# Both SwiGLU openings written out as one sequence, with the norm's token factor taken from a small load, the square roots' small steps on GpSimd, and the second FFN's block factors found inside the output projection

## The chip, the cores and the metric

The kernel runs on one core of a Trainium2 chip. The metric is the device time of one execution in microseconds (us). A core has a matrix engine (PE, which reads its stationary operand through weight loads, PEld), a vector engine (DVE), an activation engine (ACT), GpSimd (POOL) and an engine whose queue issues the DMAs (SP). Every engine works its own list of instructions in order, and waits on semaphores for the others.

## The reference

One decoder layer over 1024 tokens of width 1024, in float32:

```
x = x + 0.5 * swiglu(rms_norm(x, ffn1_norm), w_gate, w_up, w_down)      # FFN 1, hidden width 2816
p = rms_norm(x, mix_norm) @ w_in                                        # latents, q, k, v, gates
x = x + (sigmoid(g_mla) * (A @ W_A) + sigmoid(g_fox) * (B @ W_B)) @ w_o # two causal attentions
x = x + 0.5 * swiglu(rms_norm(x, ffn2_norm), w_gate, w_up, w_down)      # FFN 2
rms_norm(x, g) = x * rsqrt(mean(x*x) + 1e-6) * g
swiglu(h) = (silu(h @ w_gate) * (h @ w_up)) @ w_down
```

The change concerns the start of the two FFNs and the end of `@ w_o`.

## The kernel before

Products of float32 accuracy are made of three cheaper ones. Each operand is split in a high part and the rest (low part), and `high*high + high*low + low*high` is accumulated in PSUM. In the FFNs' first product both parts are float16, so every operand is first multiplied by a power of two: one for the tokens (from the largest absolute norm weight, `gain_scale`, L449-457) and one for each block of 128 hidden columns (from the largest absolute weight, `block_scale`, L198-217, or from the largest row sum, `pair_stat`, L713-724). A largest value per partition is spread over all partitions by a tiny matmul into a PSUM tile `mx` (`spread_max`, L185-196), and five DVE steps of one column each (`pow2`, L168-181) make the factor and its inverse from it.

An FFN's opening normalizes eight tiles of 128 tokens. For each tile, `norm_parts` (L462-514) has three steps: *scale* (L484: ACT squares and sums the row; L117-L120: a square root of one column, one step on ACT and three on DVE; L486: DVE multiplies x by it and by the norm's weights into `y`), *transpose* (L491: eight PE transposes into PSUM) and *split* (L498: ACT copies the high part; for tiles 4 to 7 also a float32 copy into `raw`; L510: DVE subtracts for the low part). `start` (L312-336) writes this out for FFN 1, and `first_half` (L338-360) for tiles 4 to 7 of both FFNs, between the products of hidden block 0 (gate and up, tokens 0 to 511; `high` L362-367, `low` L369-379).

`ffn_up` (L571-645) then does block 0 for tokens 512 to 1023 (six groups of eight matmuls), block 1 for all tokens (`proj_T`: twice 48 matmuls into `psa`), and from block 2 on one block at a time by a Strassen-like scheme of seven products of 12 matmuls each (L759, `hidden_tile`; step 0 writes `pst`, step 1 a `psb` or `psg`). Its seven token operands are the first and third quarter as they are, and five sums t1 to t4 and b22 that `token_sums` (L664-706) makes on DVE (L682 to L697) and splits (L161 on ACT, L162 on DVE). Its seven weight operands (`op`) are made by `pair_sums` (L726-754): sums on GpSimd (L735-737, L748), splits on ACT (L164) and DVE (L165). The factor of block j comes from `pair_stat(j)` (L722: ACT sums absolute values over 2048 columns), an `mx` matmul in PE's list, and `pow2`.

What sets the order: inside a `with self.in_order(...)` an engine keeps the written order; elsewhere a scheduler places the instructions by its own estimates. Before, only `start` was in such a block; `first_half` for FFN 2 and all of `ffn_up` were placed by the scheduler. A pool with a fixed count of buffers per tag also orders: `stg` (loaded weights), `whi`, `wlo`, `y` and `atp` have two each. All loads are issued by SP in list order.

For block 1 everything was found late: its weights are loaded after block 0 is under way (`w1 = self.ffn_loads(name, 1)`), their largest value is taken by two DVE reductions (L205) that stand behind block 0's and the token sums' work, and only then come factor, high part (`whi`, L164) and low part (`wlo`, L165).

The output projection (`w_o`, L1704-1715) adds `mixed @ w_o` into x, 24 matmuls for each of 8 token tiles and 2 column halves, each group read out by one DVE addition (L1715). FFN 2's block 0 factor is found between its first and its second column half.

Of the kernel before, what the change touches and what calls it, by code (L numbers as in the profile page):

```python
# [64 lines left out]
class Layer:  # L65
# [46 lines left out]
    def rsqrt1(self, ss, inv_n):  # L112
# [3 lines left out]
        v = nc.vector  # L116
        v.tensor_scalar(out=a, in0=ss, scalar1=-0.5 * inv_n, scalar2=-0.5 * EPS, op0=ALU.mult, op1=ALU.add)  # L117
# [80 lines left out]
    def block_scale(self, loads, norm, engine=None):  # L198

        box = {}  # L200
        st = self.sm.tile([P, 6], F32, tag="bst", bufs=2, name="bst")

        def biggest(after=None):
            for k, w in enumerate(loads):
                self.nc.vector.tensor_reduce(  # L205
                    out=st[:, k:k + 1], in_=w.rearrange("p k n -> p (k n)"), op=ALU.max, axis=AX.X,
                    apply_absolute_value=True,
                )
                if after is not None:
                    self.follow(after)  # L210

        def spread():
            m = st[:, 5:6]
            self.spread_max(st, len(loads), m)
            box["s"], box["inv"] = self.pow2(m, 14, st[:, 2:5], norm["inv"], engine)

        return biggest, spread, box


# [10 lines left out]
    def layer(self):  # L230
# [4 lines left out]
        self.load_x(x, src, range(1))  # L235
        norm["g"] = self.gain("ffn1_norm")
# [4 lines left out]
        first = self.start(norm, loads)  # L241
# [18 lines left out]
        pending = self.ffn_up(norm, "ffn1", first, tags)  # L260
# [32 lines left out]
        self.spare = None  # L293
# [18 lines left out]
    def start(self, norm, loads):  # L312
        ET = mybir.EngineType
        nc = self.nc
        ready = lambda t: self.norm_parts(norm, t)
        with self.in_order(ET.Activation, ET.DVE, ET.PE):

            warm = self.psg("warm")
            for k in range(20):
                nc.tensor.transpose(warm[:, (k % 4) * P:(k % 4 + 1) * P], self.ident, self.ident)  # L320
            (s0, t0, c0), (s1, t1, c1), (s2, t2, c2), (s3, t3, c3) = (ready(t) for t in range(4))
            box = []
            pg, pu = self.psbg(), self.psbg()
            pair = slice(0, 256)
            a, b = (lambda o=o, k=k: self.high(o, box[k], norm["hi"][0], pair) for k, o in enumerate((pg, pu)))

            big, spread, found = self.block_scale([l[0] for l in loads], norm)
            gs = lambda: norm.update(s=self.gain_scale(norm))
            self.spare, self.turn = self.slot("wd"), 0
            w0, w1 = (  # L330
                lambda l=l, k=k: box.append(self.col_split(l, self.spare[:, k * 1024:(k + 1) * 1024], found["s"]))
                for k, l in enumerate(loads)
            )
            for f in (s0, gs, t0, s1, t1, s2, c0, big, t2, spread, s3, c1, w0, a, w1, t3, b, c2, c3):
                f()
            norm["first"] = found["inv"]
            return self.first_half(norm, box, [ready(t) for t in range(4, NT)], (pg, pu))

    def first_half(self, norm, first, parts, begun=None):


        hT = norm["hi"], norm["lo"]
        pg, pu = begun or (self.psbg(), self.psbg())
        (s4, t4, c4), (s5, t5, c5), (s6, t6, c6), (s7, t7, c7) = parts
        hi, lo = hT[0][0], hT[1][0]
        cols = slice(256 if begun else 0, HALF)
        a, b = (lambda o=o, w=w: self.high(o, w, hi, cols) for o, w in ((pg, first[0]), (pu, first[1])))
        (ca, cb), (da, db) = (self.low(o, w, hi, lo) for o, w in ((pg, first[0]), (pu, first[1])))
        norm["ops"] = sums = self.token_sums(norm)
        d = lambda: sums[3](0)  # L350
        order = (
            (s4, a, b, ca, t4, s5, s6, c4, cb, t5, s7, c5, t6, c6, da, t7, d, c7, db)
            if begun else
            (s4, a, t4, s5, s6, c4, b, t5, c5, ca, cb, t6, s7, c6, da, t7, d, c7, db)
        )
        for f in order:
            f()
        traced = self.nc.cur_bb.bb.instructions
        self.last_act = next(i.name for i in reversed(traced) if i.engine == mybir.EngineType.Activation)
        self.last_dve = next(i.name for i in reversed(traced) if i.engine == mybir.EngineType.DVE)  # L360
        return first, (pg, pu)

    def high(self, o, w, hi, cols=slice(0, HALF)):

        for k in range(KD):
            self.nc.tensor.matmul(
                o[:, cols], lhsT=w[0][:, k, :], rhs=hi.at(k, cols), start=k == 0 and cols.start == 0, stop=False
            )

    def low(self, o, w, hi, lo):  # L370
        def first():
            for k in range(KD):
                self.nc.tensor.matmul(o, lhsT=w[1][:, k, :], rhs=hi.at(k), start=False, stop=False)

        def second():
            for k in range(KD):
                self.nc.tensor.matmul(o, lhsT=w[0][:, k, :], rhs=lo.at(k), start=False, stop=k == KD - 1)

        return first, second
# [82 lines left out]
    def norm_parts(self, st, t):  # L462


# [11 lines left out]
        box = {}  # L476

        def scale():
            if st["spill"] is not None:
                nc.sync.dma_start(st["spill"][t * P:(t + 1) * P, :], xt)  # L480
            y = box["y"] = self.ring.tile([P, D], F32, tag="y", bufs=2, name="y")
            ss = self.sm.tile([P, 1], F32, tag="ss", bufs=4, name="ss")

            nc.scalar.activation(y, xt, AF.Square, accum_out=ss)  # L484
            r = self.rsqrt1(ss, 1.0 / D)
            nc.vector.scalar_tensor_tensor(out=y, in0=xt, scalar=r, in1=st["g"], op0=ALU.mult, op1=ALU.mult)  # L486
# [6 lines left out]
        def split():  # L493
            sc, ps = st["s"] if t == 0 else None, box["ps"]

            def copy(dst, src):
                if sc is None:
                    nc.scalar.copy(dst, src)  # L498
                else:
                    nc.scalar.activation(dst, src, AF.Copy, scale=sc)  # L500

            for k in (0, 4):
                copy(h.rows(k, 4, s), ps[:, k:k + 4, :])
            if t >= 4 and st["raw"] is not None:
                for k in (0, 4):
                    copy(st["raw"].rows(k, 4, s), ps[:, k:k + 4, :])
            for k in (0, 4):
                o, a, b = l.rows(k, 4, s), ps[:, k:k + 4, :], h.rows(k, 4, s)
                if sc is None:
                    nc.vector.tensor_tensor(out=o, in0=a, in1=b, op=ALU.subtract)  # L510
# [15 lines left out]
    def col_split(self, loaded, low=None, scale=None):  # L526
        st, k0 = loaded
        dt = F32R if scale is None else F16
        hi = self.ring.tile([P, 8, P], dt, tag="whi", bufs=2, name="whi")
        lo = self.ring.tile([P, 8, P], dt, tag="wlo", bufs=2, name="wlo")  # L530
        nc = self.nc
        if scale is not None and low is not None:
            scaled = low.rearrange("p (k n) -> p k n", n=P)
            nc.scalar.activation(hi, st, AF.Copy, scale=scale)
            nc.gpsimd.tensor_scalar(out=scaled, in0=st, scalar1=scale, scalar2=None, op0=ALU.mult)
            nc.gpsimd.tensor_tensor(out=lo, in0=scaled, in1=hi, op=ALU.subtract)
            return hi, lo
# [1206 lines left out]
```

## Time and profile before

| what | us |
|---|---|
| median of 3 runs (2140.96 to 2144.5) | 2143.45 |
| the profiled execution | 2142.04 |
| its span, first to last instruction | 2140.3 |
| PE busy | 2083.4 (97%) |
| DVE busy | 1340.6 (63%) |
| ACT busy | 1051.4 (49%) |
| GpSimd busy | 701.9 (33%) |

The trace is of the profiled execution, 1.74 us longer than its span. In rows of the timeline the columns are start, duration, engine, line, operation, output<-inputs, shapes and count; a bracket gives the idle time of that engine ahead of the row and what ended it. Rows of the waits give engine, tile and line that waited, the instruction waited for, and the total, the count and the longest. Rows of the windows give the stretch, its length, each engine's busy time (instructions), PE's granted clock (1.00 is full), the DMA engines' busy share and GB/s.

### The profile page before, as it was taken

Reading aid. Unit: us, or ns where it says so; the run is one execution under the profiler, and the core shown is the slowest. Engines: PE = TensorE matmul, PEld = TensorE weight load, DVE = VectorE, ACT = ScalarE, POOL = GpSimd, SP = SyncE. Lnnn points to the kernel's source line nnn. Section 1 sums busy time; section 2 is a strip of 40 time slices with the busy share of each in tenths; the row PEclk is TensorE's granted clock in tenths of the full one; section 3 lists DMA queues with packets and bytes.
Section 4 is the critical chain, followed back from the end, with each engine's and each line's share of the span. In section 5 each row is a group of like instructions: output and inputs, shape, how many; then the busy total and the mean of one; then the engine's idle time right before and its main releaser. Section 6 shows DMA issues by size and latency. Waiting matters only on the chain.

```text
span 2140.3 us, 28367 instructions
## 1 busy us (share of the span) xinstructions
PE 2083.4 (97%) x10209; PEld 1439.9 (67%) x10209; DVE 1340.6 (63%) x2337; ACT 1051.4 (49%) x1837; POOL 701.9 (33%) x723
## 2 busy tenths in 40 slices
PE   7799999999999999999999999999899999999999
PEld 4344444457888888888888888888344444448887
DVE  7654545568776787545556677853764544559765
ACT  6355555544444554356656765422455555544442
POOL 2245555474201121123333432000155555566200
PEclk8899999999999999999999999999999999999999
DMA  7133424365434377674555684641433342455432
GB/s 212 35 99 99 151 90 130 98 251 181 138 113 146 93 218 216 206 188 138 138 144 140 182 219 120 214 150 65 113 98 109 108 129 92 141 191 202 134 107 108
DMA packets 251636, 305.39 MB, mean 143 GB/s; under 512 B 17656, under 2 KB 186472, under 8 KB 251496
## 3 DMA queue, kind: packets, MB, share of 16 engines
q1 hardware_dynamic: 251496, 303.59, 46.6%
q8 instruction: 80, 1.31, 0.3%
q14 instruction: 60, 0.49, 0.1%
HBM read 205.54 MB, written 98.00 MB: 142 GB/s over the span
## 4 chain that ended last, share of the span: by engine, by line
PE 87%; DVE 5%; DMA 2%; ACT 2%; issue 1%; POOL 1%; SPq 0%; DVEq 0%; ACTq 0%; POOLq 0%
PE pst L759 19%; PE psd L906 16%; PE psb L759 11%; PE pss L1527 4%; PE psg L759 4%; PE pspt L1553 3%; PE pspv L1564 3%; PE psgate L154 3%; PE psgate L155 3%; PE psgate L156 3%; PE psb L156 2%; PE psb L154 2%; PE psb L155 2%; PE psin L154 2%; PE psin L155 2%; PE psin L156 2%
## 5 line engine op out<-in xcount | busy, mean ns | idle before, releaser
L759 PEld LDWEIGHTS <-op 128*128 128x128 f16 x3360 | 329.1, 98 | 396.3 <-ACT op L164 6.0
L906 PE MATMUL psd<-op 128*128 128x512 f32 x1680 | 383.8, 390 | 1.8 <-DVE op L162 1.8
L906 PEld LDWEIGHTS psd<-op 128*128 128x128 f32 x1680 | 315.0, 188 | 69.5 <-DVE op L162 4.0
L759 PE MATMUL pst<-s_u,op 128*128 128x512 f16 x720 | 165.4, 379 | 3.0 <-ACT op L164 2.8
L759 PE MATMUL pst<-s_v,op 128*128 128x512 f16 x720 | 165.2, 379 | 0.0
L1534 ACT ACTIVATE s_act<-pss,nm 128x128 f32<-128x128 f32 (+7 forms) x128 | 95.0, 742 | 98.3 <-DVE nm L1531 96.1
L162 DVE TENSOR_TENSOR op<-s_u,op 128x512 fp32r<-128x512 f32 x120 | 103.9, 865 | 37.8 <-ACT op L161 37.8
L161 ACT CAST op<-s_u 128x512 fp32r<-128x512 f32 x120 | 74.4, 620 | 106.3 <-PE psd L906 91.9
L165 DVE SCALAR_TENSOR_TENSOR op<-s_act,s_wd,op 128x512 f16<-128x512 f32 x100 | 83.5, 852 | 55.0 <-ACT op L164 54.9
L165 DVE SCALAR_TENSOR_TENSOR op<-s_u,s_v,op 128x512 f16<-128x512 f32 x100 | 83.4, 852 | 53.0 <-ACT op L164 52.9
L735 POOL TENSOR_TENSOR sums<-s_u 128x512 f32<-128x512 f32 x20 | 26.3, 1315 | 271.9 <-DVE bst L175 176.0
L1527 PE MATMUL pss<-s_wd 96*128 96x256 f32 (+5 forms) x480 | 113.1, 361 | 0.4 <-DMA s_wd<-mk 0.3
L161 ACT CAST op<-s_wd 128x512 fp32r<-128x512 f32 x95 | 59.0, 621 | 106.5 <-PE psd L906 97.3
L1572 DVE TENSOR_TENSOR cmb<-pspv,cmb 64x512 f32<-64x512 f32 x64 | 44.0, 688 | 104.1 <-ACT cmb L1571 103.6
L164 ACT ACTIVATE op<-s_act,s_wd 128x512 f16<-128x512 f32 x100 | 67.9, 716 | 81.5 <-DVE s_wd L178 72.8
L164 ACT ACTIVATE op<-s_u,s_v 128x512 f16<-128x512 f32 x100 | 67.8, 716 | 79.2 <-DVE s_v L178 76.4
L162 DVE TENSOR_TENSOR op<-s_wd,op 128x512 fp32r<-128x512 f32 x95 | 80.3, 845 | 36.1 <-ACT op L161 36.1
L154 PE MATMUL psgate<-s_u,whi 128*128 128x512 f32 x256 | 101.6, 397 | 0.6 <-ACT z L1376 0.6
L1557 DVE TENSOR_TENSOR s_v<-pspt,s_v 128x512 fp32r<-128x512 f32 (+1 forms) x160 | 96.4, 632 | 7.7 <-ACT s_v L1556 6.0
L155 PE MATMUL psgate<-s_u,whi 128*128 128x512 f32 x256 | 100.8, 394 | 0.0
L156 PE MATMUL psgate<-s_u,wlo 128*128 128x512 f32 x256 | 100.5, 393 | 0.0
L1531 DVE TENSOR_REDUCE nm<-pss 128x1 f32<-128x128 f32 (+7 forms) x128 | 93.6, 750 | 1.5
(521 smaller groups left out, 4664.4 us busy)
## 6 DMA issues: line engine op xcount, KB each, us to landing
sumd<-s_u SPq DMA_DIRECT2D x20, 1024.0 KB, 5.2
sumd<-s_wd SPq DMA_DIRECT2D x13, 1024.0 KB, 5.2
s_wd<-fd SPq DMA_DIRECT2D x48, 256.0 KB, 5.4
s_u<-in_ffn_w_down_dram SPq DMA_DIRECT2D x22, 512.0 KB, 5.5
s_wd<-sumd SPq DMA_DIRECT2D x14, 768.0 KB, 4.2
s_u<-sumd SPq DMA_DIRECT2D x14, 768.0 KB, 4.4
s_act<-in_ffn_w_gate_dram SPq DMA_DIRECT2D x20, 512.0 KB, 3.9
s_act<-in_ffn_w_up_dram SPq DMA_DIRECT2D x20, 512.0 KB, 5.4
```

Of the source, the lines that this page charges most:

```text
L154: mm(out, lhsT=lh, rhs=rh, start=start, stop=False)
L155: mm(out, lhsT=lh, rhs=rl, start=False, stop=False)
L156: mm(out, lhsT=ll, rhs=rh, start=False, stop=stop)
L161: self.nc.scalar.copy(hi, src)
L162: self.nc.vector.tensor_tensor(out=lo, in0=src, in1=hi, op=ALU.subtract)
L164: self.nc.scalar.activation(hi, src, AF.Copy, scale=scale)
L165: self.nc.vector.scalar_tensor_tensor(out=lo, in0=src, scalar=scale, in1=hi, op0=ALU.mult, op1=ALU.subtract)
L759: mm(out, lhsT=a[:, k, :], rhs=b[:, k, :], start=start and k == 0 and i == 0, stop=k == n - 1 and i == 2, skip_group_check=True,)
L906: nc.tensor.matmul(o, lhsT=u[:, r], rhs=w, start=start and m == 0, stop=k == CK - 1 and m == 2, skip_group_check=True,)
L1527: mm(ps[:, b:e], lhsT=a[:, q], rhs=bb[:, b:e], start=k == 0, stop=k == len(passes) - 1)
L1534: nc.scalar.activation(pn[:, :n], ps[:, :n], AF.Exp, bias=nm, accum_out=rs[:, i, j:j + 1])
L1557: nc.vector.tensor_tensor(out=lo, in0=pt[:, s0:], in1=hi, op=ALU.subtract)
```

## The change

1. *Token factor of FFN 1.* A load of the norm's weights as 128 x 8 (`small`, 4 KB) goes second in SP's list. DVE reduces it, an `mx` matmul among PE's warm-up transposes spreads it, and the factor is made ahead of the first tile's scaling; before, it was reduced from the 128 x 1024 broadcast (`gain`, L453) behind it.
2. *Square roots.* For tiles 1 to 7 of FFN 1 the three one-column steps (L117, L119, L120) go from DVE to GpSimd. The square's elementwise output goes to a junk buffer, so it no longer holds a `y` buffer.
3. *Block 0's low part in FFN 1* goes from GpSimd (L535, L536) to DVE; its high product is made in one piece of 512 columns, no longer in pieces of 256.
4. *Written order.* `norm_steps` gives six steps (q square, s scale, t transpose, h high, r raw, l low); `start`, `first_half` and the head of `ffn_up` write them out, the latter in an `in_order` block, up to `pair_stat(3)`. In half two the order of the groups is H, H, M, M, L, L (high*high, high*low of tokens, low*high).
5. *Block 1's weights.* FFN 1: loaded after the pairs 2 to 5 (before: ahead of some of them); its factor from two ACT sums of absolute values (`sums`), no longer from DVE reductions; high and low part made during block 0's second half. FFN 2: loaded, factored and split inside the first four tiles of `w_o`, as block 0.

The core of the diff:

```diff
+    def plain(self, loads, norm, engine=None):
+        def sums():
+            for k, w in enumerate(loads):
+                nc.scalar.activation(
+                    self.spare[:, :512].bitcast(BF16), flat(w), AF.Abs, accum_out=st[:, k:k + 1]
+                )
...
+        for n, p in enumerate((p0, p1)):
+            p["biggest"]()
             for t in range(4):
                 self.w_o(x, mixed, ws, t, n)
-            if n == 0:
-                spread()
-                norm2["first"] = found["inv"]
-                first = [self.col_split(l, scale=found["s"]) for l in loads]
+            p["spread"]()
+            p["hi"]()
+            p["lo"]()
...
+        steps = lambda t: self.norm_steps(norm, t, nc.gpsimd if t else None)
...
+            go("t0", "q1", "h0", "s1", "t1", "q2", "q3", "l0", "s2", "t2")
+            p0["biggest"]()
+            go("h1", "s3")
+            p0["spread"]()
...
-        w1 = self.ffn_loads(name, 1)
-        big, spread, found = self.block_scale([l[0] for l in w1], norm)
-        big(after=self.last_dve)
-        stats[2] = stat(2)
-        nxt = self.pair_sums(loads.pop(2), stats.pop(2), norm, scales, 2)
-        sums[2]()
-        spread()
-        bg, bu = (self.col_split(l, scale=found["s"]) for l in w1)
-        sums[4]()
+            total(2)
+            high(2)
+            low(2)
+            out(1, pg, pu)
+            nxt = self.pair_sums(loads.pop(2), stats.pop(2), norm, scales, 2)
+            ops = [next(nxt) for _ in range(2)]
+            high(3, 1)
+            low(3, 1)
+            a = self.ring.tile([P, T], F32, tag="y", bufs=2, name="a")
+            nc.scalar.activation(a, p2, AF.Silu, scale=p1["inv"])
+            p3 = self.proj_T(p1["w"][1], hT)
+            total(4)
+            high(4)
+            low(4)
+            ops += [next(nxt) for _ in range(5)]
...
+            stats[3] = stat(3)
```

The engines' lists show what this moves, at three places. First ACT in FFN 1, from the first SiLU of block 0 (L600) to the statistic of pair 3, before (`s_wd<-s_act` of 2048 columns is `pair_stat`, `op` a split weight operand, `whi` block 1's high part, `CAST s_v<-s_v` of 2048 columns a large token sum's high part, t2 first and t4 second):

```order
L600 ACTIVATE a_524<-psg,bst 128x512
L161 CAST s_wd<-s_v 128x4x256
L722 ACTIVATE s_wd<-s_act 128x2048
L161 CAST s_v<-s_v 128x2048
L164 ACTIVATE whi<-stg,bst 128x1024 x2
L161 CAST s_v<-s_v 128x2048
L620 ACTIVATE a<-psa,bst 128x1024
L164 ACTIVATE op<-s_act,s_wd 128x512 x3
L164 ACTIVATE op<-sums,s_wd 128x512 x2
L164 ACTIVATE op<-s_act,s_wd 128x512 x2
L722 ACTIVATE s_wd<-s_act 128x2048
```

After the change, in the same place (`t_450` and `t_527` are small token sums; the SiLU is now L663, that of block 1 L705):

```order
L228 ACTIVATE whi<-stg,bst 128x1024 x2
L765 CAST s_wd<-s_v 128x4x256 x2
L810 ACTIVATE s_wd<-s_act 128x2048
L765 CAST s_v<-s_v 128x2048
L663 ACTIVATE a_587<-psg,bst 128x512
L164 ACTIVATE op<-s_act,s_wd 128x512 x2
L765 CAST s_wd<-t_527 128x4x256
L705 ACTIVATE a<-psa,bst 128x1024
L765 CAST s_v<-s_v 128x2048
L164 ACTIVATE op<-s_act,s_wd 128x512
L164 ACTIVATE op<-sums,s_wd 128x512
```

Block 1's high part now stands ahead of pair 2's statistic and of both large token sums; the first two operands of pair 2 stand ahead of t4's copy, the other five and pair 3's statistic behind it.

Second, DVE in `w_o` ahead of FFN 2, behind block 0's low part, before (`r1a`, `r1t`, `r1r` are the steps of a square root, `s_u<-psb,s_u` the read-out of a `w_o` group):

```order
L165 SCALAR_TENSOR_TENSOR wlo<-stg,bst,whi 128x1024 x2
L1715 TENSOR_TENSOR s_u<-psb,s_u 128x512
L117 TENSOR_SCALAR r1a<-ss 128x1
L119 TENSOR_SCALAR r1t<-r1y,r1a 128x1
L120 TENSOR_SCALAR r1r<-r1t,r1y 128x1
L486 SCALAR_TENSOR_TENSOR y<-s_u,r1r,gain 128x1024
```

And after (`bst<-stg` is the largest absolute value of one of block 1's two weight tiles):

```order
L232 SCALAR_TENSOR_TENSOR wlo<-stg,bst,whi 128x1024 x2
L1803 TENSOR_TENSOR s_u<-psb,s_u 128x512
L215 TENSOR_REDUCE bst<-stg 128x1
L117 TENSOR_SCALAR r1a<-ss 128x1
L215 TENSOR_REDUCE bst<-stg 128x1
L119 TENSOR_SCALAR r1t<-r1y,r1a 128x1
L120 TENSOR_SCALAR r1r<-r1t,r1y 128x1
L563 SCALAR_TENSOR_TENSOR y<-s_u,r1r,gain 128x1024
```

Block 1's two reductions have moved here from FFN 2's opening; its factor and low part follow some rows further down, between two later read-outs.

Third, PE in FFN 2 at the end of block 1's second projection, before (`psa` is the projection, `mx` the spread of pair 2's statistic, `pst` step 0 of pair 2):

```order
L155 MATMUL psa<-s_wd,whi 128x512
L156 LDWEIGHTS wlo
L156 MATMUL psa<-s_wd,wlo 128x512
L191 MATMUL mx<-ident,s_v 128x128
L759 LDWEIGHTS op
L759 MATMUL pst<-s_act,op 128x512
```

And after, where the spread now is, at the end of the first projection:

```order
L156 LDWEIGHTS wlo
L156 MATMUL psa<-s_wd,wlo 128x512
L191 MATMUL mx<-ident,s_v 128x128
L154 LDWEIGHTS whi
L154 MATMUL psa<-s_act,whi 128x512
L155 LDWEIGHTS whi
```

Pair 2's spread has moved ahead of the second projection's 48 matmuls. Pair 3's stays where it was: behind step 0 in FFN 1, behind step 1 in FFN 2.

More of the change, by code (lines that the diff above doesn't have):

```diff
@@ L214, in spread, with hi, lo @@
             self.spread_max(st, len(loads), m)
-            box["s"], box["inv"] = self.pow2(m, 14, st[:, 2:5], norm["inv"], engine)
-        return biggest, spread, box
+            box["s"], box["inv"] = self.pow2(m, 14, st[:, 2:5], norm["inv"])
+        def hi():
+            h, l = (self.ring.tile([P, 2, KD, P], F16, tag=t, bufs=2, name=t) for t in ("whi", "wlo"))
+            box["w"] = [(h[:, a], l[:, a]) for a in range(2)]
+            for (o, _), w in zip(box["w"], loads):
+                nc.scalar.activation(o, w, AF.Copy, scale=box["s"])
+        def lo():
+            for (h, o), w in zip(box["w"], loads):
+                nc.vector.scalar_tensor_tensor(
+                    out=flat(o), in0=flat(w), scalar=box["s"], in1=flat(h), op0=ALU.mult, op1=ALU.subtract
+                )
+        box.update(sums=sums, biggest=biggest, spread=spread, hi=hi, lo=lo)
+        return box
     def run(self):
@@ L240, in layer @@
         self.constants()
-        first = self.start(norm, loads)
+        first = self.start(norm, loads, small, tags)
         mix = self.norm_begin(None, None, ("u", "u"), spill=self.xd)
@@ L310, in layer, with start @@
         self.ffn_down(x, "ffn2", dict(raw=("act", "wd"), extra="v", acts="u"), tail2, pending)
-    def start(self, norm, loads):
+    def start(self, norm, loads, small, tags):
         ET = mybir.EngineType
         nc = self.nc
-        ready = lambda t: self.norm_parts(norm, t)
+        steps = lambda t: self.norm_steps(norm, t, nc.gpsimd if t else None)
         with self.in_order(ET.Activation, ET.DVE, ET.PE):
             warm = self.psg("warm")
[L319 to L328, printed above, removed]
-            self.spare, self.turn = self.slot("wd"), 0
[L330 to L361, printed above, removed]
@@ L363, in high, with heat @@
-    def high(self, o, w, hi, cols=slice(0, HALF)):
+            def heat(n):
+                for k in range(n):
+                    nc.tensor.transpose(warm[:, (k % 4) * P:(k % 4 + 1) * P], self.ident, self.ident)
+            heat(14)
+            self.gain_scale(norm, small)
+            norm["late"] = True
+            self.spare, self.turn = self.slot("wd"), 0
+            norm["junk"] = self.spare[:, :512].bitcast(BF16)
+            heat(6)
+            n = {t: steps(t) for t in range(4)}
@@ L365, in high, with first_half @@
         for k in range(KD):
             self.nc.tensor.matmul(
-                o[:, cols], lhsT=w[0][:, k, :], rhs=hi.at(k, cols), start=k == 0 and cols.start == 0, stop=False
+                o, lhsT=a[:, k, :], rhs=b.at(k), start=which == "H" and k == 0, stop=which == "L" and k == KD - 1
             )
[L370 to L379, printed above, removed]
+    def first_half(self, norm, p0):
+        pg, pu = self.psbg(), self.psbg()
+        n = {t: self.norm_steps(norm, t) for t in range(4, NT)}
+        (wg, wu), (hi, lo) = p0["w"], (norm[k][0] for k in ("hi", "lo"))
+        full = lambda t: [n[t][c]() for c in "hrl"]
+        both = lambda t: [n[t][c]() for c in "qs"]
+        part = lambda o, w, c: self.part(o, w, hi, lo, c)
+        both(4)
+        part(pg, wg, "H")
+        n[4]["t"]()
+        both(5)
+        both(6)
+        full(4)
+        part(pu, wu, "H")
+        n[5]["t"]()
+        full(5)
+        part(pg, wg, "M")
+        part(pu, wu, "M")
+        n[6]["t"]()
+        both(7)
+        full(6)
+        part(pg, wg, "L")
+        n[7]["t"]()
+        full(7)
+        part(pu, wu, "L")
+        self.mark()
+        return pg, pu
@@ L524, in col_load, with col_split @@
         return st, k0
[L526 removed]
+    def col_split(self, loaded, low=None):
         st, k0 = loaded
[L528 to L530 removed]
+        hi = self.ring.tile([P, 8, P], F32R, tag="whi", bufs=2, name="whi")
+        lo = self.ring.tile([P, 8, P], F32R, tag="wlo", bufs=2, name="wlo")
         nc = self.nc
[L532 to L537, printed above, removed]
[L538 to L540 removed]
         nc.scalar.copy(hi[:, :k0], st[:, :k0])
@@ L620, in ffn_up @@
-        nc.scalar.activation(a, pg, AF.Silu, scale=found["inv"])
-        pu = self.proj_T(bu, hT)
-        nc.vector.scalar_tensor_tensor(out=a, in0=pu, scalar=found["inv"], in1=a, op0=ALU.mult, op1=ALU.mult)
-        nc.sync.dma_start(dst[1], a)
-        ops = [next(nxt) for _ in range(7)]
-        stats[3] = stat(3)
+        with self.in_order(ET.Activation, ET.DVE, ET.PE):
+            out(0, *banks)
+            total(3, 0)
+            if not ready:
+                p1["sums"]()
+            pg, pu = self.psbg(), self.psbg()
+            (wg, wu), (h1, l1) = p0["w"], (h[1] for h in hT)
+            part = lambda o, w, c: self.part(o, w, h1, l1, c)
+            part(pg, wg, "H")
+            part(pu, wu, "H")
+            part(pg, wg, "M")
+            total(1, 0)
+            high(3, 0)
+            low(3, 0)
+            if not ready:
+                p1["spread"]()
+                p1["hi"]()
+                p1["lo"]()
+            part(pu, wu, "M")
+            part(pg, wg, "L")
+            part(pu, wu, "L")
+            high(1, 0)
+            low(1, 0)
+            total(3, 1)
+            total(1, 1)
+            high(1, 1)
+            low(1, 1)
+            stats[2] = stat(2)
+            p2 = self.proj_T(p1["w"][0], hT)
+            total(2)
[13 more added lines that the diff above has]
+            ops += [next(nxt) for _ in range(5)]
+            nc.vector.scalar_tensor_tensor(out=a, in0=p3, scalar=p1["inv"], in1=a, op0=ALU.mult, op1=ALU.mult)
+            nc.sync.dma_start(dst[1], a)
+            stats[3] = stat(3)
```

225 lines of the change are left out of this document (133 added, 92 removed).

## The prediction

> **What bounds the kernel now.** I read the page's busy times first, then the chain of work that ended last. PE is busy nearly all the time and makes up most of the chain, so a gain must be time in which PE waits or runs slowly.
>
> ```profile
> PE 2083.4 (97%) x10209; PEld 1439.9 (67%) x10209; DVE 1340.6 (63%) x2337; ACT 1051.4 (49%) x1837; POOL 701.9 (33%) x723
> PE 87%; DVE 5%; DMA 2%; ACT 2%; issue 1%; POOL 1%; SPq 0%; DVEq 0%; ACTq 0%; POOLq 0%
> ```
>
> Next come PE's waits in the two openings, 0 to 130 us and then 1480 to 1600 (total, count, longest).
>
> ```profile
> PE psa L154 <- ACT whi L164: 6.5, 1, 6.5
> PE psa L491 <- DVE r1a L117: 6.4, 3, 3.4
> PE mx L191 <- ACT s_wd L722: 3.4, 1, 3.4
> PE pst L759 <- ACT op L164: 2.8, 1, 2.8
> ...
> PE psa L154 <- ACT whi L164: 6.4, 1, 6.4
> PE psa L156 <- DVE wlo L165: 1.4, 1, 1.4
> ```
>
> Both openings wait most for block 1's high part, `whi`. The steps of the square root, which the waits name as `r1a`, come second, in FFN 1 alone. Of the windows (length, busy time of PE, PEld, DVE, ACT, POOL, granted clock, DMA share, GB/s) two carry something:
>
> ```profile
> 0.00:26.00 26.00, 14.96 (x68) 12.47 (x69) 16.93 (x36) 13.00 (x24) 7.84 (x30) 0.69 1.02 312
> 26.00:60.00 34.00, 26.34 (x138) 15.06 (x135) 30.82 (x41) 22.42 (x39) 3.96 (x3) 0.94 0.47 102
> ```
>
> Up to 26 us the DMA engines are full. From 26 to 60 us DVE is, at 30.82 of 34 us: there the opening goes as fast as DVE gets through its list. PE's rows in FFN 1 date the stages: half two of block 0, block 1, pair 2's spread, step 0, pair 3's spread, steps 1 to 3.
>
> ```profile
> 45.28 1.89 PE L366 MATMUL psg<-s_u,whi 128*128 128x512 f16 x8 [1.14 <-ACT s_u L498]
> 64.07 0.61 PE L154 MATMUL psa<-s_u,whi 128*128 128x512 f16 x1 [6.54 <-ACT whi L164]
> 89.32 0.38 PE L191 MATMUL mx<-ident,s_wd 128*128 128x128 f32 x2
> 92.50 0.60 PE L759 MATMUL pst<-s_u,op 128*128 128x512 f16 x2 [2.79 <-ACT op L164]
> 98.99 0.79 PE L191 MATMUL mx<-ident,s_wd 128*128 128x128 f32 x2 [3.38 <-ACT s_wd L722]
> 99.57 3.88 PE L759 MATMUL psb<-s_u,op 128*128 128x512 f16 x12
> 103.29 2.75 PE L759 MATMUL psb<-s_wd,op 128*128 128x512 f16 x12
> 105.88 2.75 PE L759 MATMUL pst<-s_v,op 128*128 128x512 f16 x12
> ```
>
> Twelve warm matmuls take 105.88 - 103.29 = 2.59 us, or 0.216 each. So 8 take 1.73, 48 take 10.35 and 96 take 20.7. From 64.07 to 89.32 stand 96 that took 25.25, because PE came out of its wait cold.
>
> **The change part by part.** I wrote out the new lists of PE, ACT and DVE with the durations of the rows, letting each instruction start when its engine and its inputs are ready. What follows are the nodes of that walk.
>
> *FFN 1, up to half two.* These rows show a square root's steps with the scaling behind them, and tile 7's way: scaling, transposes, high part.
>
> ```profile
> 30.76 0.14 DVE L117 TENSOR_SCALAR r1a<-ss 128x1 f32<-128x1 f32 x1
> 31.57 1.28 DVE L486 SCALAR_TENSOR_TENSOR y<-s_v,r1r,gain 128x1024 f32<-128x1024 f32 x1
> 37.82 1.28 DVE L486 SCALAR_TENSOR_TENSOR y<-s_v,r1r,gain 128x1024 f32<-128x1024 f32 x1
> 41.39 1.04 PE L491 MATMUL psa<-ident,y 128*128 128x128 f32 x8
> 44.65 1.07 ACT L498 CAST s_u<-psa 128x512 f16<-128x512 f32 x2
> ```
>
> The steps hold DVE for 31.57 - 30.76 = 0.81 us a tile, 5.7 for seven tiles. Going to GpSimd, they leave DVE; against that, two low-part passes over block 0's weights (about 2.5 us) come to DVE. The walk ends tile 7's scaling at 36.85, where it ended at 39.10. Its transposes then find their PSUM buffer free and nothing queued ahead of them and end at 37.75 (42.43 before), and the high part follows with no other work ahead of it on ACT: half two starts at 39.65, 5.6 earlier than 45.28. The small load and its spread cost tile 0 about 0.4 us, which the walk holds.
>
> The walk prices GpSimd's three steps like DVE's. No row shows them there. The nearest rows:
>
> ```profile
> 734.43 0.23 POOL L986 TENSOR_TENSOR rot<-s_v 128x16 f32<-128x16 f32 x1
> 1573.76 1.27 POOL L736 TENSOR_TENSOR s_u<-s_u 128x512 f32<-128x512 f32 x1
> 1525.55 3.27 POOL L736 TENSOR_TENSOR s_u<-s_u 128x512 f32<-128x512 f32 x1
> ```
>
> A small operation took 0.23 us, as on DVE; and one and the same sum took 1.27 alone but 3.27 beside DVE's two-input passes. So a set of three steps costs between nothing more than before and 3 x 1.28 = 3.8 us more, 1.28 being the DVE pass beside it that it could have to sit out. Three sets (tiles 1, 2 and 6) lie on the path: 0 to 11.5 us. I take 0.5 a set, 1.5 in all, near the small row.
>
> *FFN 1, block 1.* These rows give the prices of a pass over 2048 columns, of a copy, of `pair_stat` and of three operands:
>
> ```profile
> 1534.35 2.29 DVE L697 TENSOR_TENSOR s_u<-s_u,s_act 128x2048 f32<-128x2048 f32 x1
> 1536.67 1.90 ACT L161 CAST s_u<-s_u 128x2048 f16<-128x2048 f32 x1 [9.21 <-DVE s_u L697]
> 1518.18 1.91 ACT L722 ACTIVATE s_v<-s_u 128x2048 bf16<-128x2048 f32 x1
> 1554.92 1.95 ACT L164 ACTIVATE op<-s_u,s_v 128x512 f16<-128x512 f32 x3 [11.01 <-DVE s_v L178]
> ```
>
> Six groups of 8 end at 39.65 + 10.35 = 50.0. Block 1's factor is there at 48.2 and its high part, two ACT passes, at 50.4, so block 1 starts at 50.7 instead of 64.07: 13.4 earlier. Its wait is only 0.7, so PE stays warm, and the 96 matmuls take 20.7 instead of 25.25: 4.5 more. Pair 2's spread now stands between the projections and its first two operands are ready at 68; step 0 ends at 74.2, where it ended at 98.99 - 3.38 = 95.61: 21.4 earlier.
>
> What is late next is pair 3's spread, behind step 0. It needs `pair_stat`, which stands on ACT behind t4's copy and five operands, and that copy behind two DVE passes, which the walk starts at 70.2: 70.2 + 2 x 2.29 + 1.90 + 5 x 0.65 + 2.1 (1.91 and a read-out) = 82.0. PE waits 7.8 us there, instead of 3.38, and step 1 starts at 82.4: 17.2 ahead of 99.57. After such a wait PE is cold: the 96 matmuls above lost 25.25 - 20.7 = 4.5, and less a wait for the low part like FFN 2's 1.4 that is 3.1. Cold costs between 3.1 and 4.5 us, then; I take 3.5, as that wait was there. Before, step 1 already lost (103.29 - 99.57) - 2.59 = 1.1. So 2.4 go back: 14.8. With GpSimd's 1.5 off, FFN 1 gains 13.3.
>
> The Trainium skill ("TensorE: Matmul & The Clock Gate", Part 1, What's actually happening) says that about 3.4 us of sustained work at half clock end the cold stretch, whatever the count of matmuls. That would cost about 1.7 us, an estimate, and bring the sum to 2110.9; the trace, with at least 3.1 lost after a wait of 6.54, speaks for a longer stretch.
>
> *FFN 2.* Its rows on PE, and the two on DVE that show what stood ahead of tile 7's scaling:
>
> ```profile
> 1507.43 1.06 PE L491 MATMUL psa<-ident,y 128*128 128x128 f32 x8 [1.03 <-DVE y L486]
> 1526.48 0.61 PE L154 MATMUL psa<-s_act,whi 128*128 128x512 f16 x1 [6.35 <-ACT whi L164]
> 1552.52 0.38 PE L191 MATMUL mx<-ident,s_v 128*128 128x128 f32 x2
> 1555.69 4.51 PE L759 MATMUL pst<-s_act,op 128*128 128x512 f16 x12 [2.79 <-ACT op L164]
> 1560.04 2.75 PE L759 MATMUL psg<-s_v,op 128*128 128x512 f16 x12
> 1562.85 2.75 PE L759 MATMUL psb<-s_act,op 128*128 128x512 f16 x12
> ...
> 1502.29 1.22 DVE L682 TENSOR_TENSOR t<-s_u 128x1024 f32<-128x1024 f32 x1
> 1506.00 1.28 DVE L486 SCALAR_TENSOR_TENSOR y<-s_u,r1r,gain 128x1024 f32<-128x1024 f32 x1
> ```
>
> From 1502.29 to 1506.00 DVE made token sums between tile 7's small steps; written out, tile 7 comes first, and its transposes start near 1504.5. The table load and a SiLU stand ahead of its high part on ACT, so half two starts at 1507.6 and ends at 1517.9. Block 1's halves are ready from `w_o`: it starts at 1518.1, 8.4 earlier than 1526.48, and warm: 1552.52 - 1526.48 = 26.04 becomes 20.7, 5.3 more. The spread stands between the projections and the operands are ready at 1531, so 1555.69 - 1552.52 = 3.2 go, and step 0 takes 2.6 and not 1560.04 - 1555.69 = 4.35: 1.75. Step 1 ends near 1544.1, 18.7 earlier. Pair 3's statistic, by the same chain (t4 at 1537.5, + 1.90 + 3.25 + 2.1), is there at 1544.75, and step 2 starts at 1545.1, not 1562.85. FFN 2 gains 17.8. PE hardly waits there, as the spread stands behind step 1, not step 0.
>
> *In `w_o`* come two reductions, two high and two low passes and a spread. DVE adds one read-out of 0.69 per group and then idles 4.75:
>
> ```profile
> 1451.34 0.69 DVE L1715 TENSOR_TENSOR s_u<-psb,s_u 128x512 f32<-128x512 f32 x1 [4.75 <-PE psb L156]
> ```
>
> Each pass of some 1.2 us fits in such a gap; were it not so, a pass of 1.2 would hold PE up by at most its own length. I take the spread's 0.4 on PE.
>
> *Sum.* 13.3 + 17.8 - 0.4 = 30.7 us. The profiled execution took 2142.04; the median is 2143.45, 1.41 more, and I forecast against the median: 2112.7.
>
> **The rivals.** *GpSimd's steps are slow.* At 3.8 a set FFN 1 gains 14.8 - 11.5 = 3.3, all in all 20.7: 2122.7. For it speaks the 3.27 us row, against it the 0.23 one and that operations of one column read little. The Trainium skill ("GPSIMD Engine Reference", 1. Specifications) has GpSimd share its memory interfaces with VectorE, with contention when a DVE instruction has two inputs there; the 3.27 row agrees. Chance 0.16.
>
> *Pair 3's statistic comes in time.* If the DVE list runs ahead of my walk by the 7.8 us of the wait in FFN 1, the wait and its cold go: 7.8 + 2.4 = 10.2, 2102.5. DVE's fullness speaks against it. Chance 0.06.
>
> *The gain comes back as other waits* (this ends at no change). Were DVE to take as long for the new list as for the old up to t4's low part, step 1 would stand where it did, in both openings: 2143. Against it: the work removed from DVE is counted in rows. Chance 0.04.
>
> *Block 1's loads are late* (slower). They now stand behind eight loads of pairs. 21 loads of 0.524 MB (128 x 1024 x 4 bytes) are 11.0 MB; at 312 GB/s they land at 35 us, before the 41 us at which ACT's sums ask for them in the walk. At 102 GB/s after 26 us (2.9 MB left) they land at 54, which costs 13 of the gain. It ends slower than before only if they land after 41 + 31 = 72 us, which is below 62 GB/s; at 35 GB/s it would be 109 us, 37 behind: 2180. Against it: the 312 GB/s while loads were queued; the 102 is a mean over a window with DMA engines busy for 0.47 of it. Chance 0.03.
>
> **How the numbers follow.** Forecast 0.71, the rivals 0.16, 0.06, 0.04 and 0.03. The forecast's own bounds: 1.5 better if GpSimd's steps cost nothing, 2.4 better if cold costs no more than before, and some 6 worse if the eight tiles and the projections queue less tightly than in the walk (six waits like the 1.03 and 1.14 us of the rows). From 2112.7 that reaches to 2108.8 and 2118.7. The range from 2105 to 2125 takes in these, part of the way to the early statistic, and the slow steps with 2 us beside them; it leaves out that statistic's end and the last two rivals: 0.13 in chance. A measurement of this kernel can tell about 0.2%, 4.3 us, from no change. Faster: 0.71 + 0.16 + 0.06 = 0.93; the same 0.04; slower 0.03.
>
> **What would show it.** Right: PE's half two near 40 to 42 us, block 1 near 51 with a wait under 1 us, a wait of 6 to 8 us at pair 3's `mx` in FFN 1 with cold matmuls behind it and none to speak of in FFN 2; block 1 of FFN 2 some 8 us earlier, step 2 near 1545 less the shift of FFN 1. The one-column rows on GpSimd say at once whether they take 0.2 or 1 us. Wrong: a wait for `whi` or `wlo` that stays, a wait on the DMA of block 1's weights, or PE held up in `w_o`.

## The result and the profile after

| | us |
|---|---|
| before, median of 4 runs (2140.96 to 2144.50) | 2143.53 |
| changed, median of 4 runs (2114.02 to 2118.81) | 2116.51 |
| ratio, 95% interval | 0.9876 (0.9858 to 0.9893) |
| the profiled execution, before and after | 2142.04 and 2114.02 |
| both again, on another occasion: before, changed | 2142.58, 2116.34 |

The change takes 27 us, 1.2%, where 30.7 were forecast. PE's share of the span rises by a point, though its busy time falls by 10.6 us:

```profile
PE 2072.8 (98%) x10195; PEld 1435.6 (68%) x10195; DVE 1333.9 (63%) x2317; ACT 1052.2 (50%) x1841; POOL 702.3 (33%) x740
```

PE's waits in the two openings of the changed kernel (0 to 130 us, then 1460 to 1590) show what went and what came:

```profile
PE mx L191 <- ACT s_wd L810: 9.4, 1, 9.4
PE psa L570 <- DVE y L563: 8.9, 6, 2.4
PE psa L156 <- DVE wlo L232: 0.2, 1, 0.2
...
PE psg L847 <- DVE op L165: 1.8, 1, 1.8
PE psg L847 <- ACT op L164: 0.6, 1, 0.6
```

The waits of 6.5 and 6.4 us for block 1's high part are gone from both. In FFN 1 the wait for pair 3's statistic has grown from 3.4 to 9.4 us; in FFN 2 one of 2.4 us in all is new. PE's rows of the changed kernel, FFN 1 first: half two, block 1, pair 2's spread, step 0, pair 3's spread, step 1, step 2, pair 4's spread.

```profile
42.10 1.89 PE L391 MATMUL psg<-s_u,whi 128*128 128x512 f16 x8
52.91 0.38 PE L154 MATMUL psa<-s_u,whi 128*128 128x512 f16 x1
63.60 0.39 PE L191 MATMUL mx<-ident,s_wd 128*128 128x128 f32 x2
74.18 2.75 PE L847 MATMUL pst<-s_u,op 128*128 128x512 f16 x12
86.35 0.80 PE L191 MATMUL mx<-ident,s_wd 128*128 128x128 f32 x2 [9.41 <-ACT s_wd L810]
86.94 4.27 PE L847 MATMUL psb<-s_u,op 128*128 128x512 f16 x12
91.05 2.75 PE L847 MATMUL psb<-s_wd,op 128*128 128x512 f16 x12
106.59 0.38 PE L191 MATMUL mx<-ident,s_wd 128*128 128x128 f32 x2
```

Pair 4's spread stood at 118.83 before: FFN 1 is 12.24 us shorter. In `w_o` the read-outs that wait for PE alone stand 12.8 us earlier than before up to the eighth group and 12.35 from the ninth on, behind the spread that moved in there: it cost 0.5 us. In FFN 2:

```profile
1495.21 7.07 PE L391 MATMUL psb<-s_wd,whi 128*128 128x512 f16 x32 [0.29 <-ACT s_wd L578]
1505.57 0.38 PE L154 MATMUL psa<-s_act,whi 128*128 128x512 f16 x1
1526.51 2.75 PE L847 MATMUL pst<-s_act,op 128*128 128x512 f16 x12
1529.85 0.60 PE L847 MATMUL psg<-s_v,op 128*128 128x512 f16 x2 [0.59 <-ACT op L164]
1532.21 2.12 PE L847 MATMUL psg<-s_v,op 128*128 128x512 f16 x9 [1.76 <-DVE op L165]
1550.27 0.39 PE L191 MATMUL mx<-ident,s_v 128*128 128x128 f32 x2
```

There pair 4's spread was at 1578.39: 28.12 us earlier now, of which FFN 2 has 28.12 - 12.35 = 15.8. Behind it nothing more is gained or lost (the span is 28.1 shorter).

### The profile page after: what moved, and what is told of

It is laid out like the page before. It is cut to its first block, busy times and chain, and to the rows that moved or that the text cites. A ratio compares the mean times of both kernels' runs of the same rounds, so it can differ in the third digit from the quotient of the medians.

```text
span 2112.2 us, 28335 instructions
## 1 busy us (share of the span) xinstructions
PE 2072.8 (98%) x10195; PEld 1435.6 (68%) x10195; DVE 1333.9 (63%) x2317; ACT 1052.2 (50%) x1841; POOL 702.3 (33%) x740
## 4 chain that ended last, share of the span: by engine, by line
PE 87%; DVE 5%; ACT 3%; DMA 2%; issue 1%; POOL 1%; SPq 0%; ACTq 0%; POOLq 0%; DVEq 0%
PE pst L847 19%; PE psd L994 17%; PE psb L847 11%; PE pss L1615 4%; PE psg L847 4%; PE pspt L1641 3%; PE psgate L154 3%; PE psgate L155 3%; PE psgate L156 3%; PE pspv L1652 3%; PE psb L156 2%; PE psb L155 2%; PE psb L154 2%; PE psin L154 2%; PE psin L155 2%; PE psin L156 2%
## 5 line engine op out<-in xcount | busy, mean ns | idle before, releaser
L823 POOL TENSOR_TENSOR sums<-s_u 128x512 f32<-128x512 f32 x20 | 27.3, 1363 | 268.2 <-DVE s_wd L591 162.8
```

## The experiments

All kernels are edits of the changed one, timed beside the kernel before. Profiled executions differ by up to 6 us between the openings, in the attention part that no edit touches, so times are read with their interval and the openings by their rows.

**Block 1 late.** In both FFNs block 1's factor and parts go back behind the second half's token sums; the written order stays.

```diff
-            if not ready:
-                p1["spread"]()
-                p1["hi"]()
-                p1["lo"]()
             part(pu, wu, "M")
...
+            p1["biggest"]()
             stats[2] = stat(2)
+            p1["spread"]()
+            p1["hi"]()
+            p1["lo"]()
             p2 = self.proj_T(p1["w"][0], hT)
```

> The written order stays, but block 1's largest value, factor, high and low part are made in both FFNs where they were made before: behind the token sums of the second half, ahead of pair 2's statistic and t2. Theory (block 1's early parts are worth about half of the gain, since in FFN 1 pair 3's statistic, at 86 us, ends last anyway): FFN 1 starts block 1 near 62 instead of 52.9, but step 1 ends near 93 instead of 91.05, about 2 us lost; FFN 2 starts it some 9 us later and comes out cold, about 11 us lost; w_o gives back 0.4. Sum 12.5 us, about 2129 us. Rival (the whole gain is block 1's early factor, whose two waits were 6.5 and 6.4 us with cold matmuls behind them): at least 24 us lost, 2140 us or more. Rival (the written order does it all): less than 4 us lost.

Measured: 2134.41 us, ratio 0.9968 (0.9956 to 0.9980), against the changed kernel's 0.9876 some 20 us slower. The theory and both rivals miss. PE in FFN 1:

```profile
58.66 0.80 PE L191 MATMUL mx<-ident,bst 128*128 128x128 f32 x2 [6.06 <-DVE bst L215]
62.84 0.61 PE L154 MATMUL psa<-s_u,whi 128*128 128x512 f16 x1 [2.26 <-ACT whi L228]
75.80 0.38 PE L191 MATMUL mx<-ident,s_wd 128*128 128x128 f32 x2
93.24 0.79 PE L191 MATMUL mx<-ident,s_wd 128*128 128x128 f32 x2 [4.11 <-ACT s_wd L809]
93.82 4.99 PE L846 MATMUL psb<-s_u,op 128*128 128x512 f16 x12
98.65 2.75 PE L846 MATMUL psb<-s_wd,op 128*128 128x512 f16 x12
```

Step 1 ends at 98.65 and not near 93: 7.6 us lost where 2 were expected. The theory had overlooked that pair 2's spread now stands behind the first projection: block 1 late makes pair 2's factor late too (75.80 against 63.60), and with it the whole list of DVE up to pair 3's statistic. In FFN 2 some 11.6 us are lost, as expected. So in the written order block 1's early parts carry about 20 of the 27 us.

**Pair 3's statistic earlier.** `stats[3] = stat(3)` moves on ACT from behind pair 2's operands to ahead of t4, where ACT idles.

```diff
             p3 = self.proj_T(p1["w"][1], hT)
+            stats[3] = stat(3)
             total(4)
...
             nc.sync.dma_start(dst[1], a)
-            stats[3] = stat(3)
```

> Pair 3's statistic is moved ahead on ACT, to before t4, where ACT idles 5.9 us; no work is added or removed. Theory (that statistic, queued behind t4's copy and five operands, sets the end of FFN 1's opening): no wait at pair 3's mx, step 1 near 77 instead of 86.9; then the third operand, whose low part is ready near 84.3, ends last, so step 2 ends near 87 to 88.5 instead of 93.6: 5 to 6.6 us. In FFN 2 the scheduler now puts step 1 ahead of step 2, which hides the wait for the third operand there: about 2.2 us. Sum 7 to 9 us, 2108 to 2110 us. Rival (the operands of pair 2 end last, and the statistic only shares their time): under 3 us.

Measured: 2112.06 us, ratio 0.9861 (0.9844 to 0.9877), which overlaps the changed kernel's: about 3 us faster, where 7 to 9 were expected and the rival had under 3, so the time alone decides nothing. The rows do:

```profile
78.21 0.39 PE L191 MATMUL mx<-ident,s_wd 128*128 128x128 f32 x2
78.43 2.75 PE L847 MATMUL psb<-s_u,op 128*128 128x512 f16 x12
83.45 0.74 PE L847 MATMUL psb<-s_wd,op 128*128 128x512 f16 x2 [2.27 <-ACT op L164]
85.81 4.45 PE L847 MATMUL psb<-s_wd,op 128*128 128x512 f16 x10 [1.62 <-DVE op L165]
```

The wait of 9.4 us is gone, and 3.9 us for the third operand take its place. From half two to pair 4's spread it is 103.28 - 43.53 = 59.75 us against 106.59 - 42.10 = 64.49: 4.7 less, near the 5 expected. In FFN 2 only 0.5 of the 2.2 us came: step 1 now runs ahead of step 2, but a later step waits 2.2 us for ACT to empty its PSUM bank.

**Square roots back on DVE.** The three steps of tiles 1 to 7 stand on DVE, directly ahead of each scaling.

```diff
-            box["r"] = self.rsqrt1(ss, 1.0 / D, engine)
...
         def scale():
+                v(out=a, in0=box["ss"], scalar1=-0.5 / D, scalar2=-0.5 * EPS, op0=ALU.mult, op1=ALU.add)
+                v(out=tt, in0=y1, scalar1=y1, scalar2=a, op0=ALU.mult, op1=ALU.mult)
+                v(out=r, in0=tt, scalar1=1.5, scalar2=y1, op0=ALU.add, op1=ALU.mult)
```

> The one-column steps of the square roots of tiles 1 to 7 of FFN 1 go back from GpSimd to DVE, each set directly ahead of its scaling. Theory (0.35 us a set is lost in the hand-over to GpSimd on the sets that end last, about what DVE gains elsewhere): half two within 1 us of 42.1, the whole within 1 us of the changed kernel. Rival (DVE is the bound up to half two, so the 0.81 us a set comes back whole): half two 5 us later, the whole 4 to 6 us slower. Rival (GpSimd's steps sit out DVE's passes and cost 1 us a set or more): 2 us or more faster.

Measured: 2118.55 us, ratio 0.9893 (0.9878 to 0.9908); by time it can't be told from the changed kernel's 0.9876. Half two starts at 45.61, 3.5 us later, of which 0.9 was there at the first scaling already (7.97 against 7.06, a load). So by the rows of this one profile the steps on GpSimd are worth about 2.6 us of the opening: more than the theory said, which misses, and less than the first rival's 5. The second rival falls.

**One sum from GpSimd to DVE.**

```diff
-        pool(out=a12, in0=a12, in1=s2, op=ALU.subtract)
+        (pool if j != 2 else nc.vector.tensor_tensor)(out=a12, in0=a12, in1=s2, op=ALU.subtract)
```

> One sum of pair 2's operands, which GpSimd makes beside t4's first pass, goes to DVE ahead of that pass (0.7 us more on DVE). Theory (the two slow each other): t4's first pass takes 2.3 us as in the kernel before instead of 3.35, in both FFNs; t4's copy is 0.4 us earlier, the whole 0 to 1 us faster. Rival (the longer pass has another cause): the pass stays at 3.35 us and the whole is 1 to 1.4 us slower.

Measured: 2113.71 us in one run. The changed kernel's rows first, on DVE t4's first pass and the pass ahead of it, and the sum beside them on GpSimd:

```profile
72.57 1.23 DVE L769 TENSOR_TENSOR s_wd<-t,s_wd 128x1024 f16<-128x1024 f32 x1
73.72 3.35 DVE L785 TENSOR_TENSOR s_v<-s_u,s_v 128x2048 f32<-128x2048 f16 x1
72.58 2.34 POOL L836 TENSOR_TENSOR s_act<-s_act,sums 128x512 f32<-128x512 f32 x1 [5.98 <-DVE op L165]
```

And with the sum on DVE:

```profile
72.39 0.69 DVE L838 TENSOR_TENSOR s_act<-s_act,sums 128x512 f32<-128x512 f32 x1
74.14 2.28 DVE L785 TENSOR_TENSOR s_v<-s_u,s_v 128x2048 f32<-128x2048 f16 x1
```

The pass is back at 2.28 us, in FFN 2 too (2.29). The two engines do slow each other, by 1.07 us each here (the sum takes 1.27 alone). The ends fit turns: the sum, begun with the pass of L769, ends 1.1 us behind it, and t4's pass some 2.2 us behind the sum. Pair 3's wait ends 0.5 us sooner, counted from half two, but step 1 then took 4.63 us instead of 4.11, and pair 4's spread stands 64.48 us behind half two, against 64.49.

**The head left to the scheduler.** The `in_order` block of the second part binds no engine any more; what is asked for, and in which program order, stays.

```diff
-        with self.in_order(ET.Activation, ET.DVE, ET.PE):
+        with self.in_order():
             out(0, *banks)
```

> The head of the FFNs' second part is no longer held to the written order: the scheduler places ACT's, DVE's and PE's instructions from the first SiLU up to pair 3's statistic, as before the change; block 1's weights, factor and parts are asked for as early as in the changed kernel. Theory (block 1's early factor and parts carry some 20 us of the gain, and the order itself little): block 1 starts within 2 us of 52.9 in FFN 1 and without a wait for its high part in FFN 2, the whole up to 4 us slower than the changed kernel. Rival (without the written order the early parts stand behind token sums again): waits for block 1's high or low part of 3 us or more come back, the whole 8 us or more slower.

Measured: 2108.31 us, ratio 0.9840 (0.9823 to 0.9856): about 8 us *faster* than the changed kernel, which neither theory had. PE and DVE in FFN 1:

```profile
56.04 0.39 PE L154 MATMUL psa<-s_u,whi 128*128 128x512 f16 x1 [1.12 <-ACT whi L228]
82.50 0.49 PE L191 MATMUL mx<-ident,s_wd 128*128 128x128 f32 x2 [2.14 <-ACT s_wd L810]
...
66.51 2.29 DVE L785 TENSOR_TENSOR s_v<-s_u,s_v 128x2048 f32<-128x2048 f16 x1
68.92 2.28 DVE L786 TENSOR_TENSOR s_v<-s_v,s_u 128x2048 f32<-128x2048 f32 x1
```

Block 1 waits a little again (1.6 us in all), but t4's two passes are done at 71.2, 27.3 us behind half two (43.95); in the changed kernel they end at 79.4, 37.3 behind it:

```profile
77.10 2.29 DVE L786 TENSOR_TENSOR s_v<-s_v,s_u 128x2048 f32<-128x2048 f32 x1
81.36 2.29 DVE L769 TENSOR_TENSOR s_v<-s_v 128x2048 f16<-128x2048 f32 x1 [1.96 <-ACT s_v L765]
```

The scheduler makes t4 ahead of pair 2's operands and fills DVE's waits for ACT's copies with other passes. Pair 4's spread comes 58.7 us behind half two instead of 64.5. In FFN 2 no wait is left behind half two, and its opening is 1.5 us shorter.

**Three edits together.** The early statistic, the sum on DVE, and the small load behind the broadcast (below).

> Three edits at once on the changed kernel: pair 3's statistic ahead of t4, pair 2's one GpSimd sum beside t4 on DVE, and the small load behind the broadcast of the norm's weights, with the token factor made behind the first tile's scaling. Theory (the three are independent): in FFN 1 pair 4's spread near 100 to 101 instead of 106.6, FFN 2's opening 0.5 to 1.5 us shorter, the whole 6 to 8 us faster than the changed kernel. Rival (ACT's and DVE's lists give back in pair 2's products what they gain ahead of them): under 4 us.

Measured: 2108.18 us, ratio 0.9839 (0.9824 to 0.9854), 8 us faster than the changed kernel; pair 4's spread at 100.99, FFN 2's opening 1.0 us shorter. As the theory said, in the sum; the small load shows no part in it, as the first scaling, at 6.94, still waited 0.52 us for the broadcast, and half two starts at 42.60.

**A warm wait.** 80 transposes of `ident` fill the wait at pair 3's spread.

```diff
+        for k in range(fill):
+            self.nc.tensor.transpose(ps[:, P + (k % 3) * P:P + (k % 3 + 1) * P], self.ident, self.ident)
```

> 80 idle transposes fill PE's wait at pair 3's mx in FFN 1, so that PE stays warm; they write where nothing reads. Theory (the wait's cold costs 1.5 us, step 1's 4.11 against 2.59 us): step 1 takes 2.6 us and everything behind it is 1.5 us earlier. Rival (the prediction's price): 3 us or more earlier. Rival (the clock isn't what lengthens step 1): step 1 still takes about 4.1 us.

Measured: one run, 2117.89 us. Its rows:

```profile
76.53 8.90 PE L191 MATMUL mx<-ident 128*128 128x128 f32 x80
86.45 2.75 PE L852 MATMUL psb<-s_u,op 128*128 128x512 f16 x12
89.04 2.75 PE L852 MATMUL psb<-s_wd,op 128*128 128x512 f16 x12
```

Step 1 takes 2.59 us at a granted clock of 1.00, where the changed kernel had 0.50 from 85 to 90 us. Pair 4's spread comes at 104.58, counted from half two 1.8 us earlier, and 2.2 against the changed kernel's second profile. The cold behind this wait costs 1.5 to 2.2 us, not the 3 of the rival. (This execution then lost 5.9 us in the attention part: block 1 of FFN 2 starts at 1509.43, not 1505.57.)

**The small load second.**

```diff
+        norm["g"] = self.gain("ffn1_norm")
         small = self.sm.tile([P, KD], F32, tag="tk8", bufs=1, name="tk8")
         self.nc.sync.dma_start(small, self.i["ffn1_norm"][0].rearrange("(p k) -> p k", k=KD))
-        norm["g"] = self.gain("ffn1_norm")
...
             go("q0", "s0")
+            self.gain_scale(norm, small)
             self.scale_gain(norm)
```

> The small load goes behind the broadcast of the norm's weights, and the token factor is made behind the first tile's scaling; the rest is the changed kernel. Theory (the small load holds back the broadcast, which the first scaling waits for): the first scaling starts near 6.5 instead of 7.06 to 8.0, half two 0.5 to 1.4 us earlier. Rival (something else holds the first scaling): no change at it.

Measured: one run, 2114.09 us. The first scaling starts at 6.60, waiting 0.19 for the broadcast; with the small load ahead it stood between 6.99 and 8.43 in nine profiles, in four of them behind a wait for the broadcast. In the other five it waited for no load: DVE's small steps, those of the token factor now among them, end just before it. With the three edits together, where the small load stands behind too, it started at 6.94. So in four of nine profiles the broadcast came later than in any of the three kernels that load it first; that the small load is the reason is likely, not shown. Half two starts at 41.95, against 42.10 and, in the changed kernel's second profile, 41.58: an earlier first scaling brought nothing there.

**Scheduler and early statistic.**

> Two edits together on the changed kernel: the head of the FFNs' second part is left to the scheduler, and pair 3's statistic is asked for ahead of t4. Theory (left to the scheduler, PE's only large wait in FFN 1 behind half two is the 2.1 us for pair 3's statistic, with 1.7 us of cold matmuls behind it): no wait there, step 1 takes 2.6 us, and the whole is 3 to 5 us faster than with the scheduler alone, 11 to 12.5 us faster than the changed kernel. Rival (as with the written order, the third operand then ends last): under 2 us beyond the scheduler alone.

Measured: 2105.57 us, ratio 0.9828 (0.9813 to 0.9842), the fastest of all, 10.8 us ahead of the changed kernel beside it. In FFN 1 no wait is left at pair 3's spread:

```profile
78.85 0.38 PE L191 MATMUL mx<-ident,s_wd 128*128 128x128 f32 x2
79.07 2.75 PE L847 MATMUL psb<-s_u,op 128*128 128x512 f16 x12
81.66 2.75 PE L847 MATMUL psb<-s_wd,op 128*128 128x512 f16 x12
```

Pair 4's spread comes 98.32 - 42.62 = 55.7 us behind half two, 3.0 less than with the scheduler alone; by the ratios it is 2.6 us, a little short of the 3 to 5 expected, and there the intervals overlap.

**The changed kernel again.**

> The changed kernel itself, unedited, beside the run above on the same chip. All theories: half two near 42 to 44, a wait of 9 us at pair 3's mx in FFN 1, a ratio of 0.986 to 0.989 to the kernel before.

Measured: 2116.34 us, ratio 0.9879 (0.9862 to 0.9895); half two at 41.58, the same wait of 9.4 us, pair 4's spread at 106.49.

## Why the prediction was right, and where its steps were off

The mechanism held in its main steps: the median lies 3.8 us above the forecast of 2112.7 and inside the range. The gain by stages, forecast and measured: FFN 1 13.3 and 12.2; `w_o` -0.4 and -0.5; FFN 2 17.8 and 15.8, or 14.2 in the changed kernel's second profile.

- *Up to half two.* Forecast 39.65, or 41.15 with the 1.5 us set aside for GpSimd; measured 42.10 and 41.58. GpSimd's sets were priced about right: one takes 10.60 - 9.45 = 1.15 us to the scaling, 0.34 more than on DVE, where 0.5 was taken. The walk let tile 7's scaling end at 36.85. It ended at 39.33, as it stands on DVE behind tile 5's low part, and that behind a copy on ACT:

```profile
36.85 1.29 DVE L591 TENSOR_TENSOR s_u<-psa,s_u 128x512 f16<-128x512 f32 x2 [1.20 <-ACT s_v L585]
38.06 1.27 DVE L563 SCALAR_TENSOR_TENSOR y<-s_v,r1r,gain 128x1024 f32<-128x1024 f32 x1
```

- *Block 1 early and warm.* Right: the two waits are gone, and 96 matmuls take 74.18 - 52.91 = 21.3 us with the spread, where 20.7 and the spread were forecast. Put late again, it took back 20 us.
- *Pair 3's spread is late next.* Right, and its size too small: 9.4 us where 7.8 were forecast, at 86.35 and not 82.0. Of the 4.3 us some 2.4 were there at half two, 1.1 is t4's first pass beside GpSimd's sum, and the rest DVE's waits for ACT's copies. With the statistic earlier the wait went.
- *The cold behind it.* Forecast 3.5 us, measured 1.5 here, 1.95 in the second profile, 1.5 to 2.2 by the warm wait. The term was taken from block 1 of the kernel before, and misread there: the prediction took off FFN 2's wait of 1.4 us for the low part, but FFN 1 had one of its own, of 1.71.

```profile
67.85 0.61 PE L156 MATMUL psa<-s_u,wlo 128*128 128x512 f16 x1 [1.71 <-DVE wlo L165]
```

  So 25.25 - 20.7 - 1.71 = 2.8 us were lost in that place, not at least 3.1; in FFN 2 it was 26.04 - 20.7 - 1.4 = 3.9. The price of a cold start is not the same from place to place. The Trainium skill's 3.4 us of work at half clock ("TensorE: Matmul & The Clock Gate", Part 1, What's actually happening), which would be 1.7 us, an estimate, came nearer than my row. The 2.0 us too much in this term and the 1.5 set aside for GpSimd offset most of the 4.3 us by which pair 3's spread was late: that FFN 1 came within 1.1 us of its forecast is in part luck.
- *FFN 2.* Up to step 0 all nodes came within 0.2 us (half two at 1495.21 + 12.35 = 1507.56 against 1507.6, block 1 at 1517.9 against 1518.1). The step that failed is "PE hardly waits there": what stands ahead of pair 3's spread is the step that needs pair 2's *third* operand, whose low part is queued on DVE behind t4's, and t4 again had a first pass of 3.35 us. PE waited 2.35 us for it. In the second profile the same wait was followed by slow matmuls, which took 1.5 us more:

```profile
1533.43 3.32 PE L847 MATMUL psg<-s_v,op 128*128 128x512 f16 x9 [1.76 <-DVE op L165]
```

- *The rivals.* GpSimd's steps of more than 1 us all met a DVE pass with two inputs in SBUF, mostly off the path:

```profile
25.06 2.48 DVE L232 SCALAR_TENSOR_TENSOR wlo<-stg,bst,whi 128x1024 f16<-128x1024 f32 x2
25.42 2.17 POOL L119 TENSOR_SCALAR r1t<-r1y,r1a 128x1 f32<-128x1 f32 x1 [0.28 <-ACT r1y L118]
28.90 1.28 DVE L563 SCALAR_TENSOR_TENSOR y<-s_v,r1r,gain 128x1024 f32<-128x1024 f32 x1 [0.17 <-POOL r1r L120]
```

  2.17 us beside block 0's low part, 0.34 else, and the scaling lost 0.17. The step ends 0.05 us behind that pass. Beside DVE passes with one input in PSUM (L591, L593), or with one input alone (L215), the steps took 0.19 to 0.34 us as ever. The contention that the Trainium skill names ("GPSIMD Engine Reference", 1. Specifications) was there, in these steps and in the longer DVE pass at t4. Block 1's loads never held up PE. But one sign that the prediction gave for being wrong did appear: in `w_o` DVE's two reductions waited for block 1's weights.

```profile
1418.89 1.22 DVE L215 TENSOR_REDUCE bst<-stg 128x1 f32<-128x1024 f32 x1 [1.46 <-DMA stg<-in_ffn_w_gate_dram]
1422.14 1.22 DVE L215 TENSOR_REDUCE bst<-stg 128x1 f32<-128x1024 f32 x1 [1.96 <-DMA stg<-in_ffn_w_up_dram]
```

  The read-out behind them came 2.9 us late, and PE did not wait for it. That the gain comes back as other waits was true in part: 6 us of it in FFN 1, by the written order.

What stays open: which piece of the written order costs the 8 us. The rows point to t4 and DVE's unfilled waits; the pieces weren't tried one by one. Nor were block 0's low part on DVE and its high product in one piece undone by themselves, so no run here shows what they are worth.

## What to carry to other kernels

An early input pays only as far as the queues behind it let it: here finding block 1's factor early was worth some 20 us, and fixing the order of three engines by hand at the same time gave about 8 back; by the rows DVE then waited for ACT's copies with other passes at hand. After such a change, look at the wait that has grown, follow the engine that ends it backwards, and move what stands there for no reason (one statistic ahead of five operands took the 9.4 us away, of which 4.7 were gained). The hand walk through the lists was good to a fifth of a microsecond in FFN 2 up to step 0, and 2 to 4 us short in FFN 1, where DVE and ACT hand work to and fro.

## What the runs showed of the hardware

- A GpSimd sum of 128x512 between two DVE passes with two inputs in SBUF went from 1.27 to 2.34 us, the second pass, of 128x2048, from 2.28 to 3.35: by their ends they took turns. One-column steps on GpSimd went from 0.19 to 1.12 and from 0.34 to 2.17 us beside such passes, and stayed at 0.19 to 0.34 beside passes with one input in PSUM.
- Twelve matmuls after a wait took 2.59 us plus 1.5 to 2.2 where the wait was 4.1 to 9.5 us long, with no order by its length (4.83 us after 4.1, 4.11 after 9.4). Shorter waits could cost as much: 1.7 us behind one of 2.14 (the head left to the scheduler, granted clock 0.50 from 83.5 to 86.5 us), while behind the same 1.76 us in FFN 2 of the changed kernel one profile lost nothing, at a clock of 1.00, and the other 1.5 us.
- With a load of 4 KB queued ahead of it, a 0.5 MB broadcast was waited for in four of nine profiles, until 7.17 to 8.43 us; loaded first, it was there by 6.50, 6.60 and 6.94 in three.
